# Second projection of a feed-forward block: operand loads issued three steps ahead from five buffers, and the last part's token blocks taken one at a time

## The chip, the cores and the metric

The kernel runs on one core of a Trainium2 chip. The metric is the device time of one execution in microseconds (us). The core has engines with instruction queues of their own: PE (matrix multiplies, with its weight loads), DVE, ACT and POOL (elementwise work), and SP, whose queue issues the transfers (DMA) between the chip's memory and the on-chip buffer. Each queue works strictly in the order of its list: an instruction that has to wait holds everything behind it in the same list.

## The reference

The kernel is one layer of an encoder trunk. The change touches the end of the layer, the second matrix multiply of the feed-forward block, with the residual and the layer norm behind it:

```
h = silu(x @ w_gate) * (x @ w_up)
x = LN(alpha * x + h @ w_down)        # 1024 tokens of the prompt, 128 sample tokens, D_MODEL 1024
```

All numbers are fp32. Each operand is split into a high and a low half, and each product is made of three matmuls (high by high, high by low, low by high).

## The kernel before

The second projection is `second_projection` (L1140 to L1257). It runs at the end of the program, from 1403 us of the profiled span. It uses a fast scheme for two-by-two block matrices with seven products in place of eight: for every pair of 128-row slices of the inner dimension there are seven operands of the tokens (B11, T1, T2, B22, T3, B21, T4, stored in `h_scratch` by the stage before) and seven of the weights (A11, S1, S2, S4, S3, A12, A22).

The 11 pairs are taken in five parts (`PARTS`): four of two pairs, then one of three. The tokens are in four blocks. In a part the blocks (0, 1) go through all seven steps together, then the sample tokens are done (`sample`), then the blocks (2, 3) go through the seven steps. In the last part, behind the sample, block 2 goes alone and then block 3 alone. Each step of two blocks in a part of two pairs is 12 matmuls of 128x512, a step of one block in the last part is 9.

For each step `operand` (L1146) issues the transfer of the operand into `hq` (two buffers), ACT copies it to `hh` (high half) and DVE (B11, T2, B22, B21) or POOL (T1, T3, T4) makes `hl` (low half). `hh` and `hl` have five buffers each. The step's result stands in one of two PSUM banks for each of the names x, z and w, and `add` (L1156) adds it to the sum `y` in the on-chip buffer: DVE does so at L1164, and for the w step ACT copies it to `tap` (L1161) and POOL adds it (L1162). In the last part DVE adds all of it and takes the statistics (L1168). Steps 1, 3, 5 and 7 of a block go on in the same x bank, so PE may begin such a step only when DVE has read the bank.

The weights of the next part are made beside this by `prepare` (L1103): for each pair two transfers of 512 KB into `raw` (L1108), sums on POOL (L1111 to L1114), high halves on ACT and low halves on DVE or, for A21 and A22, POOL (L1121, L1122). The odd pairs' `raw` has a single buffer, so its next transfer waits for POOL's last low half of the pair before.

`final_norm` (L1081) normalizes a finished block in the last part, on DVE, POOL and ACT, and its stores (L1097) go through SP's list too.

The order within each engine's list is fixed when the program is built. The order of SP's list decides which transfers wait behind which.

Of the kernel before, what the change touches and what calls it, by code (L numbers as in the profile page):

```python
# [9 lines left out]
F32 = mybir.dt.float32  # L10
F32R = mybir.dt.float32r
# [3 lines left out]
ALU = mybir.AluOpType  # L15
# [3 lines left out]
P = 128  # L19
# [15 lines left out]
PARTS = ((0, 2), (2, 4), (4, 6), (6, 8), (8, 11))  # L35
# [67 lines left out]
def trunk(ctx, tc, I, O):  # L103
    nc = tc.nc
    V, S, G = nc.vector, nc.scalar, nc.gpsimd
# [16 lines left out]
    def bank(name):  # L122
        return pp[name][0].tile([P, 512], F32, name=name, tag=(pp[name] + (name,))[2], bufs=pp[name][1])
# [28 lines left out]
    def mm3(out, a, b, start, stop, **kw):  # L152
        T.matmul(out, a[0], b[0], start=start, stop=False, **kw)
        T.matmul(out, a[0], b[1], start=False, stop=False, **kw)
        T.matmul(out, a[1], b[0], start=False, stop=stop, **kw)
# [77 lines left out]
    xs, hs = both[:, :1024].rearrange("p (k c) -> p k c", k=KT), both[:, 1024:]  # L233
# [672 lines left out]
    OPS = ("B11", "T1", "T2", "B22", "T3", "B21", "T4")  # L906

    h_dram = nc.dram_tensor("h_scratch", (2, len(OPS), P, PAIRS, 2, P), F32, kind="Internal").ap()
# [10 lines left out]
    def unit(c, name, dt=F32):  # L919
        return c.tile([P, 2048], dt, name=name, tag="u", bufs=14)  # L920
# [219 lines left out]
    def second_projection(f2, c, ahead, prepared, prepare):  # L1140
# [2 lines left out]
        sums = [bank("s") for _ in range(2)]  # L1143
        gb = []

        def operand(i0, i1, bs, o):  # L1146

            k, n, c = i1 - i0, len(bs), bs[0] % 2
            lo, q, hi = (f2.tile([P, 3, 2, P], t, name=x, bufs=m)[:, :k, :n]
                         for x, t, m in (("hl", F32R, 5), ("hq", F32, 2), ("hh", F32R, 5)))  # L1150
            nc.sync.dma_start(out=q, in_=h_dram[bs[0] // 2, OPS.index(o), :, i0:i1, c:c + n])
            S.copy(hi, q)  # L1152
            (G if o in ("T1", "T3", "T4") else V).tensor_tensor(lo, q, hi.bitcast(F32), op=ALU.subtract)
            return [[(hi[:, i, b], lo[:, i, b]) for i in range(k)] for b in range(n)]

        def add(b, e, half, ps, bn, which):  # L1156
            hs = slice(half * 512, half * 512 + 512)
            key = (b, e, half)
            if which == "w" and bn is None:
                t = f2.tile([P, 512], F32, name="tap", bufs=2)  # L1160
                S.copy(t, ps)  # L1161
                G.tensor_tensor(y[b, e][:, hs], y[b, e][:, hs], t, op=ALU.add)  # L1162
            else:
                V.scalar_tensor_tensor(y[b, e][:, hs], y[b, e][:, hs], 1.0 if key in y else ALPHA, ps,  # L1164
                                       op0=ALU.mult, op1=ALU.add)
            y[key] = True
            if bn is not None:
                V.bn_stats(bn[:, half], y[b, e][:, hs])  # L1168

        steps = (("x", "A11", "B11", True, (0, 0, None)),  # L1170
                 ("z", "S1", "T1", True, (1, 1, None)),
                 ("x", "S2", "T2", False, (1, 0, None)),
                 ("z", "S4", "B22", False, (1, 0, 1)),
                 ("x", "S3", "T3", False, (1, 1, 1)),
                 ("w", "A12", "B21", True, (0, 0, 0)),
                 ("x", "A22", "T4", False, (0, 1, 0)))

        def blocks(part, bs, gb):

            ws = [prepared[i] for i in range(*part)]  # L1180
            bk = {}
            bn = {(b, e): sm.tile([P, 2, 6], F32, name="bn", bufs=6) for b in bs for e in range(2)} if gb else {}
            for which, w, h, start, (e, half, fin) in steps:
                for b, hs in zip(bs, ahead.pop((bs[0] + part[0], h), None) or operand(*part, bs, h)):
                    if start:
                        bk[which, b] = bank(which)
                    ps = bk[which, b]
                    for n, wk in enumerate(ws):
                        mm3(ps, hs[n], wk[w], start and n == 0, n == len(ws) - 1, skip_group_check=not start)
                    add(b, e, half, ps, None if fin is None else bn.get((b, fin)), which)  # L1190
                    if gb and (w == "S3" or w == "A22"):
                        final_norm(y[b, fin], gb, bn[b, fin], b, fin)
                    yield

        def sample_operands(part):
            out = []
            for i in range(*part):
                q, hi, lo = (f2.tile([P, 2, P], t, name=x, bufs=2) for x, t in (("hs", F32), ("hsh", F32R), ("hsl", F32R)))
                nc.sync.dma_start(out=q, in_=hs_dram[:, i])
                split(q, hi, lo)  # L1200
                out.append((hi, lo))
            return out
# [19 lines left out]
        for n, part in enumerate(PARTS):  # L1222
            last = n == len(PARTS) - 1
            if n == 0:
                for e in range(2):
                    for b in range(2):
                        nc.sync.dma_start(out=y[b, e], in_=x2_dram[TILES[b + 4 * e]])
            if last:
                both = unit(c, "ln_gb").rearrange("p (n x) -> p n x", n=2)
                gb = [both[:, n] for n in range(2)]  # L1230
                for n in range(2):
                    nc.sync.dma_start(out=gb[n], in_=I["ln"][4 + n:5 + n, :].broadcast_to([P, D]))
            yield from blocks(part, (0, 1), gb)
            hs = sample_operands(part)
            if n == 0:
                for e in range(2):
                    for b in range(2, 4):
                        nc.sync.dma_start(out=y[b, e], in_=x2_dram[TILES[b + 4 * e]])

            while len(prepared) < min(part[1] + 1, PAIRS):  # L1240
                more()
            yield from sample(part, hs, n == 0, last)
            if last:
                ys = unit(c, "ys")[:, :1024]
                nc.sync.dma_start(out=ys, in_=x2_dram[SAMPLE])
                bn = sm.tile([P, 2, 6], F32, name="bn", bufs=6)
                for half in range(2):
                    c2 = slice(half * 512, half * 512 + 512)
                    V.scalar_tensor_tensor(ys[:, c2], ys[:, c2], ALPHA, sums[half], op0=ALU.mult, op1=ALU.add)
                    V.bn_stats(bn[:, half], ys[:, c2])  # L1250
                final_norm(ys, gb, bn, None, None)
                for b in (2, 3):
                    yield from blocks(part, (b,), gb)
                return
            while len(prepared) < PARTS[n + 1][1]:
                more()
            yield from blocks(part, (2, 3), gb)  # L1257
# [209 lines left out]
```

## Time and profile before

| | |
|---|---|
| median of 3 runs | 1707.23 us (1706.56 to 1713.33) |
| profiled execution, its own time | 1704.64 us |
| profiled execution, span | 1702.9 us |
| PE busy | 1620.7 us, 95% of the span |
| DVE, ACT, POOL busy | 67%, 40%, 29% |

The own time is 1.7 us longer than the span, and 2.6 us shorter than the median of the runs. The busy shares are averages over stages with different limits: the second projection is about 300 us long, from 1403 us, and PE has more idle time there than the average says.

### The profile page before, as it was taken

The page shows a single profiled execution, that of the slowest core. Times are in us where ns is not written, and L with a number is a line of the kernel's source. Part 1 is how long each engine was busy: PE and PEld are TensorE (multiplying, and loading weights), DVE is VectorE, ACT ScalarE, POOL GpSimd, SP SyncE. Part 2 cuts the span into 40 slices and gives each one's busy share as a digit, 9 for nine tenths or more (in the row PEclk, how much of TensorE's full clock was granted, in tenths as well). Part 3 has the DMA queues.
Part 4 walks back from the last instruction along what each step waited for, and adds up shares of the span by engine and source line. Part 5 has one row for each costly group of instructions (what it writes and reads, how often), then busy time and mean ns, then how long its engine had stood idle before and what let it go on. Part 6 is the DMA issues. An engine that isn't in the chain of part 4 may idle for free.

```text
span 1702.9 us, 24403 instructions
## 1 busy us (share of the span) xinstructions
PE 1620.7 (95%) x9065; PEld 1391.3 (82%) x9065; DVE 1134.6 (67%) x2021; ACT 674.4 (40%) x1365; POOL 495.7 (29%) x381
## 2 busy tenths in 40 slices
PE   8999999999999999999979999999999969988896
PEld 7998999999888987889877888888888857766674
DVE  6786788778488666786687454544444665767576
ACT  4543555446443544325263333323222333434321
POOL 1111111111000000000074443332333454676555
PEclk9999999999999999999998999999999988999998
DMA  7443343334974687556362333122222245333342
GB/s 239 143 160 122 102 148 104 98 118 137 314 274 154 197 278 268 198 171 236 115 205 78 104 115 117 66 74 86 95 92 96 93 164 180 105 118 118 103 146 95
DMA packets 114358, 247.91 MB, mean 146 GB/s; under 512 B 11840, under 2 KB 58048, under 8 KB 114240
## 3 DMA queue, kind: packets, MB, share of 16 engines
q1 hardware_dynamic: 114240, 246.36, 43.8%
q8 instruction: 71, 1.16, 0.3%
q14 instruction: 47, 0.39, 0.1%
HBM read 203.65 MB, written 42.60 MB: 145 GB/s over the span
## 4 chain that ended last, share of the span: by engine, by line
PE 77%; DVE 7%; DMA 6%; POOL 5%; ACT 2%; issue 2%; SPq 1%; POOLq 0%; ACTq 0%; DVEq 0%
PE a L96 48%; PE b L96 20%; PE x L96 3%; PE b L100 2%; DMA hq<-h_scratch 2%; PE z L96 1%; DVE w L1122 1%; PE s L96 1%; DMA raw<-in_w_f_dram 1%; PE w L96 1%; DVE y L1164 1%; DMA w_raw<-in_w_out_dram 1%; DMA w_raw<-in_w_fm_dram 1%; DMA w_raw<-in_w_f_dram 1%; DVE w_lo L137 1%
## 5 line engine op out<-in xcount | busy, mean ns | idle before, releaser
L137 DVE TENSOR_TENSOR w_lo<-w_raw,w_hi 128x1024 fp32r<-128x1024 f32 (+1 forms) x169 | 204.8, 1214 | 115.0 <-ACT w_hi L136 114.6
L136 ACT CAST w_hi<-w_raw 128x1024 fp32r<-128x1024 f32 (+1 forms) x169 | 174.6, 1034 | 206.1 <-PE a L96 77.4
L96 PE MATMUL a<-w_hi,q_hi 128*128 128x256 f32 (+1 forms) x576 | 197.4, 344 | 0.8 <-ACT kv_sb L270 0.7
L96 PE MATMUL a<-w_lo,q_hi 128*128 128x256 f32 (+1 forms) x576 | 196.9, 342 | 0.0
L96 PE MATMUL a<-w_hi,q_lo 128*128 128x256 f32 (+1 forms) x576 | 194.7, 338 | 0.0
L96 PE MATMUL a<-q_hi,w_hi 128*128 128x384 f32 x528 | 186.8, 354 | 7.3 <-ACT q_hi L136 4.3
L96 PE MATMUL a<-q_hi,w_lo 128*128 128x384 f32 x528 | 179.9, 341 | 0.0
L96 PE MATMUL a<-q_lo,w_hi 128*128 128x384 f32 x528 | 179.5, 340 | 0.0
L96 PE MATMUL x<-w,hh 128*128 128x512 f32 x344 | 115.0, 417 | 39.5 <-DVE y L1164 23.6
L137 DVE TENSOR_TENSOR w_lo<-a,w_hi 128x1024 fp32r<-128x1024 f32 x43 | 75.0, 1743 | 76.9 <-ACT w_hi L136 76.9
L96 PEld LDWEIGHTS a<-w_hi,q_hi 128*128 128x128 f32 x576 | 108.4, 188 | 15.6 <-ACT kv_sb L270 1.1
L96 PEld LDWEIGHTS a<-w_lo,q_hi 128*128 128x128 f32 x576 | 108.6, 189 | 13.3 <-issue 1.2
L96 PEld LDWEIGHTS a<-w_hi,q_lo 128*128 128x128 f32 x576 | 108.5, 188 | 12.7 <-issue 0.2
L96 PEld LDWEIGHTS x<-w,hh 128*128 128x128 f32 x344 | 66.6, 198 | 62.8 <-ACT hh L1152 15.7
L96 PEld LDWEIGHTS a<-q_hi,w_hi 128*128 128x128 f32 x528 | 100.5, 190 | 12.2 <-ACT q_hi L136 4.6
L699 POOL TENSOR_TENSOR rs<-rs,mhalf 128x1 f32<-128x1 f32 x18 | 17.2, 958 | 301.0 <-DVE rs L698 301.0
L96 PE MATMUL a<-T_h,w_hi 128*128 128x512 f32 x264 | 104.7, 396 | 0.0
L96 PE MATMUL a<-T_l,w_hi 128*128 128x512 f32 x264 | 104.7, 396 | 0.0
L96 PE MATMUL a<-T_h,w_lo 128*128 128x512 f32 x264 | 104.6, 396 | 0.0
L96 PEld LDWEIGHTS a<-q_lo,w_hi 128*128 128x128 f32 x528 | 100.7, 191 | 1.6 <-issue 0.9
L96 PEld LDWEIGHTS a<-q_hi,w_lo 128*128 128x128 f32 x528 | 100.2, 190 | 1.0 <-DVE w_lo L137 0.7
L1152 ACT CAST hh<-hq 128x512 fp32r<-128x512 f32 (+2 forms) x75 | 46.3, 619 | 133.2 <-DMA hq<-h_scratch 117.3
(308 smaller groups left out, 3930.4 us busy)
## 6 DMA issues: line engine op xcount, KB each, us to landing
a<-in_w_f_dram SPq DMA_DIRECT2D x44, 512.0 KB, 5.2
w_raw<-in_w_fm_dram SPq DMA_DIRECT2D x41, 512.0 KB, 3.9
h_scratch<-w_raw SPq DMA_DIRECT2D x55, 256.0 KB, 2.2
hq<-h_scratch SPq DMA_DIRECT2D x54, 256.0 KB, 2.7
w_raw<-in_w_tm_dram SPq DMA_DIRECT2D x24, 512.0 KB, 3.5
w_raw<-in_w_out_dram SPq DMA_DIRECT2D x24, 512.0 KB, 5.7
w_raw<-in_w_mq_dram SPq DMA_DIRECT2D x24, 512.0 KB, 4.2
w_raw<-in_w_mo_dram SPq DMA_DIRECT2D x24, 512.0 KB, 4.4
```

Source lines behind the costliest of these rows:

```text
L96: return self.eng.matmul(out, lhsT, rhs, **kw)
L100: return self.eng.transpose(out, in_, identity)
L136: S.copy(hi, src)
L137: V.tensor_tensor(lo, src, hi.bitcast(F32), op=ALU.subtract)
L699: G.tensor_tensor(rs, rs, mhalf[:, 0:1], op=ALU.pow)
L1122: (G if name in ("A21", "A22") else V).tensor_tensor(lo, src, hi.bitcast(F32), op=ALU.subtract)
L1152: S.copy(hi, q)
L1164: V.scalar_tensor_tensor(y[b, e][:, hs], y[b, e][:, hs], 1.0 if key in y else ALPHA, ps, op0=ALU.mult, op1=ALU.add)
```

## The change

There is one list, `wanted`, of all operands in the order in which the steps use them. At each step `operand` calls `load` for this step and the next three and `part_of` (the split into `hh` and `hl`) for this step and the next one. `hq` has five buffers of 512 elements to a partition, where there were two of 768, and `hh` and `hl` have five of 512 each in place of five of 768. In the last part the blocks 0 and 1 go singly as well, so seven transfers of 384 KB become fourteen of 192 KB.

```diff
-        def operand(i0, i1, bs, o):
-
-            k, n, c = i1 - i0, len(bs), bs[0] % 2
-            lo, q, hi = (f2.tile([P, 3, 2, P], t, name=x, bufs=m)[:, :k, :n]
-                         for x, t, m in (("hl", F32R, 5), ("hq", F32, 2), ("hh", F32R, 5)))
-            nc.sync.dma_start(out=q, in_=h_dram[bs[0] // 2, OPS.index(o), :, i0:i1, c:c + n])
-            S.copy(hi, q)
-            (G if o in ("T1", "T3", "T4") else V).tensor_tensor(lo, q, hi.bitcast(F32), op=ALU.subtract)
-            return [[(hi[:, i, b], lo[:, i, b]) for i in range(k)] for b in range(n)]
+        turns = [(part, bs) for part in PARTS[:-1] for bs in ((0, 1), (2, 3))] + [(PARTS[-1], (b,)) for b in range(4)]
+        wanted = [(*part, bs, step[2]) for part, bs in turns for step in steps][2:]
+        loaded, parted = {}, {}
+
+        def load(n):
+            if n < len(wanted) and n not in loaded:
+                i0, i1, bs, o = wanted[n]
+                k, m, c = i1 - i0, len(bs), bs[0] % 2
+                q = f2.tile([P, 512], F32, name="hq", bufs=5)[:, :k * m * P].rearrange("p (i b x) -> p i b x", b=m, x=P)
+                nc.sync.dma_start(out=q, in_=h_dram[bs[0] // 2, OPS.index(o), :, i0:i1, c:c + m])
+                loaded[n] = q
+
+        def part_of(n):
+            if n < len(wanted) and n not in parted:
+                i0, i1, bs, o = wanted[n]
+                k, m, q = i1 - i0, len(bs), loaded[n]
+                hi, lo = (f2.tile([P, 512], F32R, name=x, bufs=5)[:, :k * m * P].rearrange("p (i b x) -> p i b x", b=m, x=P)
+                          for x in ("hh", "hl"))
+                S.copy(hi, q)
+                (G if o in ("T1", "T3", "T4") else V).tensor_tensor(lo, q, hi.bitcast(F32), op=ALU.subtract)
+                parted[n] = [[(hi[:, i, b], lo[:, i, b]) for i in range(k)] for b in range(m)]
+
+        used = [0]
+
+        def operand():
+            n = used[0]
+            used[0] += 1
+            for x in range(n, n + 4):
+                load(x)
+            for x in range(n, n + 2):
+                part_of(x)
+            return parted.pop(n)
...
-                for b, hs in zip(bs, ahead.pop((bs[0] + part[0], h), None) or operand(*part, bs, h)):
+                for b, hs in zip(bs, ahead.pop((bs[0] + part[0], h), None) or operand()):
...
-            yield from blocks(part, (0, 1), gb)
+            for bs in ((0,), (1,)) if last else ((0, 1),):
+                yield from blocks(part, bs, gb)
```

SP's list at the change from the first part to the second, before. 13433, 13455, 13477 and 13497 are B11, T1, T2 and B22 of the second part's blocks (0, 1); raw2_13594 and raw2_13646 are the weights of pairs 4 and 5.

```order
L1151 DMA hq_13433<-h_scratch 128x512
L1151 DMA hq_13455<-h_scratch 128x512
L1108 DMA raw2_13646<-in_w_f2_dram 128x1024
L1108 DMA raw2_13594<-in_w_f2_dram 128x1024
L1151 DMA hq_13477<-h_scratch 128x512
L1151 DMA hq_13497<-h_scratch 128x512
L1108 DMA raw2_13594<-in_w_f2_dram 128x1024
L1108 DMA raw2_13646<-in_w_f2_dram 128x1024
```

The same place in the changed kernel. 13442, 13464, 13486 and 13506 are B22, T3, B21 and T4 of the same blocks, 13526 is B11 of the blocks (2, 3); raw2_13604 and raw2_13656 are pairs 4 and 5.

```order
L1164 DMA hq_13442<-h_scratch 128x512
L1223 DMA hs_13990<-hs_scratch 128x256
L1164 DMA hq_13464<-h_scratch 128x512
L1108 DMA raw2_13656<-in_w_f2_dram 128x1024
L1108 DMA raw2_13604<-in_w_f2_dram 128x1024
L1164 DMA hq_13486<-h_scratch 128x512
L1164 DMA hq_13506<-h_scratch 128x512
L1108 DMA raw2_13604<-in_w_f2_dram 128x1024
L1164 DMA hq_13526<-h_scratch 128x512
L1108 DMA raw2_13656<-in_w_f2_dram 128x1024
```

The operands stand three places earlier against the weights: T2 and B22 were behind the first two weight transfers and are ahead of them now, and pair 4's second weight transfer is still behind two operand loads. On ACT, DVE and POOL the rows of these parts keep their order.

SP's list near the end of the last part, before. `out` rows are stores of finished blocks (13036 and 13037 of blocks 0 and 1, 13042 of block 2, `ys` of the sample); 15122, 15139, 15156, 15172, 15189, 15220 and 15238 are the seven operands of block 3 in the order of the steps.

```order
L1097 DMA out_0_dram<-y_13037 128x512 x2
L1095 DMA out_0_dram<-ys_14949 128x512 x2
L1151 DMA hq_15122<-h_scratch 128x3x128
L1151 DMA hq_15139<-h_scratch 128x3x128
L1151 DMA hq_15156<-h_scratch 128x3x128
L1151 DMA hq_15172<-h_scratch 128x3x128
L1097 DMA out_0_dram<-y_13042 128x512 x2
L1151 DMA hq_15189<-h_scratch 128x3x128
L1151 DMA hq_15220<-h_scratch 128x3x128
L1151 DMA hq_15238<-h_scratch 128x3x128
```

The same place in the changed kernel. 15058 and 15074 are the last two operands of block 2; 15091, 15122, 15140, 15173, 15190, 15207 and 15223 are the seven of block 3.

```order
L1164 DMA hq_15058<-h_scratch 128x3x128
L1164 DMA hq_15074<-h_scratch 128x3x128
L1164 DMA hq_15091<-h_scratch 128x3x128
L1097 DMA out_0_dram<-y_13041 128x512 x2
L1164 DMA hq_15122<-h_scratch 128x3x128
L1164 DMA hq_15140<-h_scratch 128x3x128
L1097 DMA out_0_dram<-y_13037 128x512 x2
L1095 DMA out_0_dram<-ys_15001 128x512 x2
L1164 DMA hq_15173<-h_scratch 128x3x128
L1164 DMA hq_15190<-h_scratch 128x3x128
L1164 DMA hq_15207<-h_scratch 128x3x128
L1164 DMA hq_15223<-h_scratch 128x3x128
L1097 DMA out_0_dram<-y_13042 128x512 x2
```

Block 3's first three loads stood behind the sample's stores and stand ahead of them now; its last three stood behind block 2's first stores and now stand ahead of those too.

## Rows read from the trace of the kernel before

**Rows 1.** Windows by stage: length; busy us of PE, PEld, DVE, ACT, POOL; clock; DMA.

```profile
1403.10:1469.50 66.40, 58.40 (x222) 44.95 (x222) 44.88 (x56) 24.41 (x45) 38.70 (x27) 0.91 0.47 152
1469.50:1522.10 52.60, 46.70 (x192) 35.60 (x192) 35.20 (x47) 19.82 (x36) 33.66 (x23) 1.00 0.36 115
1522.10:1575.00 52.90, 48.45 (x192) 37.78 (x192) 35.83 (x47) 19.66 (x36) 33.64 (x23) 0.94 0.36 115
1575.00:1613.10 38.10, 32.60 (x138) 25.92 (x138) 22.22 (x31) 12.88 (x23) 21.33 (x15) 1.00 0.38 114
1613.10:1654.60 41.50, 39.86 (x162) 31.51 (x163) 32.15 (x53) 12.12 (x20) 23.98 (x18) 0.96 0.43 136
1654.60:1692.40 37.80, 32.23 (x127) 23.87 (x125) 26.87 (x49) 8.14 (x14) 19.15 (x17) 0.95 0.28 95
```

**Rows 2.** Waits from 1395 to 1703 us: total us, times, longest.

```profile
ACT hh L1152 <- DMA hq<-h_scratch: 117.3, 31, 9.6
PE x L96 <- DVE y L1164: 23.6, 14, 5.6
```

**Rows 3.** PE's timeline, 1403 to 1470 us: start, duration, instruction, idle time before it.

```profile
1403.14 2.07 PE L96 MATMUL x<-w,hh 128*128 128x512 f32 x4 [15.24 <-ACT hh L1152]
...
1425.08 0.63 PE L96 MATMUL x<-w,hh 128*128 128x512 f32 x2
...
1432.21 0.70 PE L96 MATMUL x<-w,hh 128*128 128x512 f32 x2 [1.35 <-DVE y L1164]
...
1439.36 1.22 PE L96 MATMUL z<-w,hh 128*128 128x512 f32 x2 [2.70 <-DVE y L1164]
```

**Rows 4.** Timelines of ACT, POOL and SP around the first change of part.

```profile
1434.95 0.62 ACT L1152 CAST hh<-hq 128x512 fp32r<-128x512 f32 x1 [1.09 <-DMA hq<-h_scratch]
1435.48 1.66 ACT L1121 CAST w<-s 128x512 fp32r<-128x512 f32 x3
...
1442.42 0.81 SPq L1108 DMA_DIRECT2D raw<-in_w_f_dram  x2
...
1445.75 0.90 SPq L1108 DMA_DIRECT2D raw<-in_w_f_dram  x2
...
1451.67 1.72 POOL L1111 TENSOR_TENSOR s<-raw 128x512 f32<-128x512 f32 x1
```

**Rows 5.** Timelines of SP, ACT, POOL and PE around the second change of part.

```profile
1497.11 0.90 SPq L1108 DMA_DIRECT2D raw<-in_w_f_dram  x2
...
1500.60 0.62 ACT L1152 CAST hh<-hq 128x512 fp32r<-128x512 f32 x1 [5.27 <-DMA hq<-h_scratch]
...
1501.78 1.28 POOL L1162 TENSOR_TENSOR y<-y,tap 128x512 f32<-128x512 f32 x1 [5.08 <-ACT tap L1161]
1503.05 1.70 POOL L1111 TENSOR_TENSOR s<-raw 128x512 f32<-128x512 f32 x1
...
1522.13 0.73 PE L96 MATMUL x<-w,hh 128*128 128x512 f32 x2 [1.65 <-DVE y L1164]
```

**Rows 6.** DMA issues from 1497.05 to 1497.40 us: size, us to landing.

```profile
raw<-in_w_f_dram SPq DMA_DIRECT2D x1, 512.0 KB, 5.9
```

**Rows 7.** Timelines of POOL and PE at the change to the last part.

```profile
1606.51 1.28 POOL L1111 TENSOR_TENSOR s<-raw 128x512 f32<-128x512 f32 x1 [0.97 <-DMA raw<-in_w_f_dram]
...
1613.19 1.19 PE L96 MATMUL x<-w,hh 128*128 128x512 f32 x2 [5.57 <-DVE y L1164]
```

**Rows 8.** Timelines of PE, SP and ACT in the last part.

```profile
1660.07 0.74 PE L96 MATMUL x<-w,hh 128*128 128x512 f32 x2 [1.06 <-DVE y L1164]
...
1680.35 0.70 PE L96 MATMUL z<-w,hh 128*128 128x512 f32 x2 [1.77 <-DVE y L1164]
...
1685.82 0.71 PE L96 MATMUL x<-w,hh 128*128 128x512 f32 x2 [1.84 <-DVE y L1164]
...
1678.72 5.11 SPq L1151 DMA_DIRECT2D hq<-h_scratch  x3
...
1681.84 0.51 ACT L1152 CAST hh<-hq 128x384 fp32r<-128x384 f32 x1 [7.03 <-DMA hq<-h_scratch]
```

More of the change, by code (lines that the diff above doesn't have):

```diff
@@ L1144, in second_projection @@
         gb = []
-        def operand(i0, i1, bs, o):
-            k, n, c = i1 - i0, len(bs), bs[0] % 2
-            lo, q, hi = (f2.tile([P, 3, 2, P], t, name=x, bufs=m)[:, :k, :n]
-                         for x, t, m in (("hl", F32R, 5), ("hq", F32, 2), ("hh", F32R, 5)))
-            nc.sync.dma_start(out=q, in_=h_dram[bs[0] // 2, OPS.index(o), :, i0:i1, c:c + n])
-            S.copy(hi, q)
-            (G if o in ("T1", "T3", "T4") else V).tensor_tensor(lo, q, hi.bitcast(F32), op=ALU.subtract)
-            return [[(hi[:, i, b], lo[:, i, b]) for i in range(k)] for b in range(n)]
+        steps = (("x", "A11", "B11", True, (0, 0, None)),
+                 ("z", "S1", "T1", True, (1, 1, None)),
+                 ("x", "S2", "T2", False, (1, 0, None)),
+                 ("z", "S4", "B22", False, (1, 0, 1)),
+                 ("x", "S3", "T3", False, (1, 1, 1)),
+                 ("w", "A12", "B21", True, (0, 0, 0)),
+                 ("x", "A22", "T4", False, (0, 1, 0)))
@@ L1168, in add @@
                 V.bn_stats(bn[:, half], y[b, e][:, hs])
[L1170 to L1176, printed above, removed]
         def blocks(part, bs, gb):
```

## The prediction

> **What bounds the kernel now.** PE is 95% busy over the span, so I first look for the stages where it is not. The windows by stage [rows 1] show it: from 1469.5 us a part of two pairs takes 52.6 us, for 192 matmuls. At full clock 24 matmuls run from 1425.08 to 1430.86 us, where PE falls idle [rows 3], 0.24 us each, so 192 are 46 us, and each such part holds some 6.6 us of stall. The first part with its surroundings is worse, and the last part (1613.1 to 1692.4, 289 matmuls, 69.4 us of work) takes 79.3.
>
> Next, who is waited for [rows 2]. ACT stands 117 us waiting for operand transfers (`hq`), far the longest entry, yet PE waits for something else: 23.6 us for DVE's y additions. So a late `hq` costs time only where ACT, behind it DVE, and behind that a y addition come late in turn. I follow that by place, since every list is in order: a y addition on DVE stands behind low halves of operands and of weights, and those behind ACT and POOL.
>
> *First part, blocks (2, 3).* Here `hq` decides. PE stalls 1.35 and 2.70 us for y, and behind the second the first two matmuls take 1.22 us against 0.63 at 1425.08 [rows 3]: the clock fell to its half level for a while. ACT waits for `hq` until 1434.95 and only then makes the weights' halves (1435.48). POOL's low halves follow, and SP can issue the next weights at 1442.42 and, behind two operand loads, at 1445.75; POOL's first sum over them is at 1451.67 [rows 4].
>
> *Second and third change of part.* Two chains arrive together. POOL idles 5.08 us for a `tap` that ACT could not copy because it waited 5.27 us for `hq`; that addition ends at 1503.06. But the weight transfer issued at 1497.11 [rows 5] takes 5.9 us to land [rows 6], so at 1503.0, and POOL's sum begins at 1503.05. From that sum to the end of the stalls (1522.13) POOL, ACT and DVE work through the weights, with PE's y additions between.
>
> *Change to the last part.* POOL's sum waits for `raw` itself (0.97 us, 1606.51) and PE restarts 6.7 us later, after its longest gap, 5.57 us [rows 7].
>
> *Last part.* PE stalls 1.06, 1.77 and 1.84 us [rows 8], among smaller ones. The last comes from the list of SP: three loads of block 3 are issued from 1678.72 on, behind stores, ACT gets the first at 1681.84 after 7.03 us, then DVE splits it and adds y.
>
> **The change part by part.** The order of ACT, DVE and POOL in the parts of two pairs is as before, and so is the arithmetic; what moves is SP's list, three steps.
>
> *Start.* The 15.24 us ahead of 1403.14 [rows 3] stay: ACT waits there for the first operand, behind the loads of `y`, and those still stand ahead of it. Gain 0.
>
> *First part.* Loads come early, so both stalls and the half clock go, and ACT can make the weights' halves when PE has finished S1, at 1430.9, not 1435.5: 4.6 us earlier. POOL's low halves and the first weight transfers then come at about 1437. The second ones were also held by an operand's buffer, until 1445.75. In the new order pair 4's second transfer still stands behind two operand loads (B21 and T4), but those use buffers freed by halves of B11 and T1, of which only T1's, on POOL, comes near; I put it at 1438.5. Plus 5.9 us [rows 6] that is 1444.4, and POOL's sum, behind the two `tap` additions, at about 1445.5 in place of 1451.67. All behind it follows: 6.2 us, of which I take 6.0. Bounds: 0, if the transfer that was issued at 1445.75 does not move; 6.7, if the sum is made at 1445.0.
>
> *Second and third change.* The `hq` wait goes, but the weight transfer does not: it is tied to POOL's low halves of the pair before. It gains only what it waited behind the operand's buffer, about 0.6 us of which I count 0.5 each, so 1.0 in all. PE's early gaps close and come back as one longer gap, ahead of the same weights. Bounds: 0 and 5.1 (half of the 5.08 that POOL idles, 2.54, at either change, if the weights land earlier too because fewer operand loads share the way).
>
> *Change to the last part.* The operands around `raw` are half as large. I take 1.0 of the 5.57; bounds 0 and 2.0.
>
> *Last part.* 79.3 less 69.4 is 9.9 us, of which about 1.3 belong to the half clock just behind 1613.19 and stay (the first two matmuls take 1.19 there [rows 7], 0.56 more than at 1425.08; 1.3 is an estimate for the stretch). 8.6 can go: block 3's loads now stand ahead of block 2's stores. Against it, blocks taken singly have less cover: between two steps that go on in one x bank stands one step of 9 matmuls (2.2 us), not three. In blocks 2 and 3 such a wait is 1.06 where nothing of `hq` was late [rows 8]. I charge one such stall for blocks 0 and 1 together: 8.6 - 1.1 is 7.5. DVE does not become the bound by its load: 32.15 and 26.87 us of 79.3, plus 1.5 us as fourteen small halves cost more than seven large [rows 1]. Bounds: 1.0, if blocks 0 and 1 lose as much as blocks 2 and 3 did (37.8 less 30.2 for 126 matmuls, 7.6), to 8.6.
>
> The end behind PE's last matmul, 10.5 us of norm and store, stays.
>
> **Sum.** 6.0 + 1.0 + 1.0 + 7.5 is 15.5. The profiled execution's own time, 1704.64, becomes 1689.1. The median is 2.6 above that execution, so I forecast 1691.7.
>
> **A rule that speaks against it.** The trace shows a gap of 2.70 us with the half clock behind it, and one of 5.57 too [rows 3, 7]; at 1522.13, behind 1.65 us, two matmuls take 0.73 and the clock stays up [rows 5]. So closing several short gaps and leaving one long one can cost clock. The Trainium skill ("TensorE: Matmul & The Clock Gate", section "HAM oscillation — how this bites in real kernels") says the same of loops: a wait for a transfer sends the engine back to half clock, and the stretch behind it pays, each time anew. By that rule the second and third change would each lose what the first matmuls after 1613.19 lose, 1.3 us, and more if the half clock lasts as it does behind 1439.36.
>
> **The rivals.** *The first part does not move.* If the weights' second transfer or another queue place holds POOL's sum at 1451.7, the stalls only shift, and 9.5 remains: 1697.7, or 1701 if the last part gives half. For it: in the later parts just this happens. Against: there the transfer was issued without a late operand ahead of ACT, in the first part the whole chain starts 4.6 us late.
>
> *Operands decide at every change.* If the weights land earlier once fewer operand loads contend, 2.54 in place of 0.5 at each of two changes and 2.0 in place of 1.0 at the last: 1691.7 - 4.1 - 1.0 is 1686.6, and 1681.5 with the whole 5.08 at both. For it: both chains end within 0.05 us of each other in rows 5, so neither is seen alone.
>
> *The clock falls at the long gaps.* 1.3 to 3 us at up to three places: 1693 to 1700. Against: behind the gap POOL's chain, not PE, sets the end, and a slower PE is partly hidden.
>
> *Slower: the x bank.* With single blocks each of 12 returns to an x bank (three in each of four blocks) must find DVE's y addition done within 2.2 us, and DVE may hold it with a norm or a low half. If every return waits 2 us, that is 24 us in place of the 8.6 that can go: 15.4 lost in the last part. With the 8.0 gained ahead of it the time is 1714.6, with nothing gained there 1722.6. It is slower by over 0.5% from 2.1 us a return in the first case ((8.6 + 8.0 + 8.5) / 12), from 1.4 us in the second. The returns in blocks 2 and 3 that are seen to wait cost 1.06 to 1.84 and most cost nothing, which speaks against it.
>
> **How the numbers follow.** 0.5%, about what a measurement of this kernel can tell from no change, is 8.5 us: faster means under 1698.7. The forecast (1687 to 1697) has 0.48, operands deciding everywhere 0.14, the clock 0.14 (0.11 of it still faster), the first part unmoved 0.18 (a third of it faster, since the last part would more likely give less than more), the x bank 0.06. That gives faster 0.79, same 0.15, slower 0.06. The range leaves out the x bank, the far end of the unmoved first part, and a gain above 24 us: 1683 to 1701.
>
> **What would show it.** Right: ACT's wait for `hq` falls from 117 to under 40 us after 1410 us; the stalls of 1.35 and 2.70 and the half clock behind them are gone; POOL's first sum behind the first part comes some 6 us earlier, the distance between such sums of consecutive parts stays within 1 us of 51.4 (1451.67 to 1503.05); the stalls at a change stand in one piece of 3 to 5 us; blocks 2 and 3 run in under 33 us. Wrong: the sums' distances shrink by 2 us or more (operands decided), or do not move at all; PE waits for y at the third, fifth or seventh step of blocks 0 and 1.

## The result, and the profile after

The changed kernel takes 1695.64 us (median of 7 runs, 1692.0 to 1700.13), the kernel before 1708.47 (7 runs, 1706.56 to 1713.33). The ratio is 0.9925, with a 95% interval from 0.9912 to 0.9938: 12.8 us less, where 15.5 were forecast.

The two profiled executions differ by less, 1695.47 against 1704.64. PE reaches the projection's first step behind the start at 1408.64 us in the changed kernel and at 1403.14 before [rows 3], and the gap ahead of it is nearly the same. So the changed kernel's profiled execution had lost 5.1 us before that gap began. I don't put this down to the change: over all kernels below the first step lies between 1396 and 1409 us, and with six buffers, in two kernels that differ only in `hq`, 5.45 us apart. From here to the end of the span it is 299.8 us before and 285.0 in the changed kernel, 14.8 less. So I compare stages, not whole executions.

PE's timeline of the changed kernel, the main rows with idle time ahead of them (start, duration, instruction, idle time):

```profile
1408.64 2.07 PE L96 MATMUL x<-w,hh 128*128 128x512 f32 x4 [15.64 <-ACT hh L1173]
...
1441.77 0.73 PE L96 MATMUL z<-w,hh 128*128 128x512 f32 x2 [1.48 <-DVE y L1196]
...
1455.75 0.73 PE L96 MATMUL x<-w,hh 128*128 128x512 f32 x2 [2.23 <-DVE y L1196]
...
1469.64 0.73 PE L96 MATMUL x<-w,hh 128*128 128x512 f32 x2 [1.08 <-DVE y L1196]
...
1506.52 0.73 PE L96 MATMUL x<-w,hh 128*128 128x512 f32 x2 [2.65 <-DVE y L1196]
...
1521.49 0.73 PE L96 MATMUL x<-w,hh 128*128 128x512 f32 x2 [1.65 <-DVE y L1196]
...
1558.39 0.73 PE L96 MATMUL x<-w,hh 128*128 128x512 f32 x2 [2.67 <-DVE y L1196]
...
1608.99 1.19 PE L96 MATMUL x<-w,hh 128*128 128x512 f32 x2 [4.12 <-DVE y L1196]
...
1633.93 0.71 PE L96 MATMUL z<-w,hh 128*128 128x512 f32 x2 [1.28 <-DVE y L1196]
...
1673.99 0.70 PE L96 MATMUL z<-w,hh 128*128 128x512 f32 x2 [1.26 <-DVE y L1196]
```

The 1.35 and 2.70 of the first part [rows 3] are one stall of 1.48 now, and no half clock follows: matmuls in pairs take 0.73 there, not 1.22. At the change to the second part 2.23 and 1.08 are left. Not shown above: between the 2.65 and the 1.65 of the second change PE also waits 0.23 and 0.75 us, and 1.09 behind the 2.67 of the third. The 5.57 ahead of the last part [rows 7] is 4.12. In the last part there is a new stall of 1.28 in block 1; of those in blocks 2 and 3 [rows 8] one of 0.31 and one of 1.26 are left.

The waits of the changed kernel from 1395 us on (who waited for whom: total us, times, longest):

```profile
ACT hh L1173 <- PE x L96: 46.2, 20, 4.1
...
PE x L96 <- DVE y L1196: 15.7, 8, 4.1
...
ACT hh L1173 <- DMA hq<-h_scratch: 9.9, 1, 9.9
```

ACT's 117.3 us of waiting for operands [rows 2] have become one wait at the start. What ACT waits for now is PE, that is, a free `hh` buffer. POOL's first sums over new weights show who comes last at a change of part:

```profile
1452.03 1.30 POOL L1111 TENSOR_TENSOR s<-raw 128x512 f32<-128x512 f32 x1 [2.38 <-DMA raw<-in_w_f_dram]
1453.29 1.26 POOL L1194 TENSOR_TENSOR y<-y,tap 128x512 f32<-128x512 f32 x1
...
1502.81 1.29 POOL L1111 TENSOR_TENSOR s<-raw 128x512 f32<-128x512 f32 x1 [2.81 <-DMA raw<-in_w_f_dram]
...
1554.68 1.28 POOL L1111 TENSOR_TENSOR s<-raw 128x512 f32<-128x512 f32 x1 [2.83 <-DMA raw<-in_w_f_dram]
...
1601.81 1.29 POOL L1111 TENSOR_TENSOR s<-raw 128x512 f32<-128x512 f32 x1 [3.46 <-DMA raw<-in_w_f_dram]
```

At each of the four POOL now stands waiting for the weights alone. Before, POOL's sum at 1503.05 came right behind a late `tap` addition [rows 5].

For all kernels the stages are measured between the starts of the sample's matmuls, which have a fixed place between the blocks (0, 1) and the next ones of each part. So the stretch from one sample to the next holds a change of part. From here on the first part is the stretch from sample 1 to 2, with the first change; the third part is the one from sample 2 to 3, with the second change, and the fourth the one from sample 3 to 4, with the third change. In us, worked out from the timelines:

```
                 start to  sample 1  sample 2  sample 3  sample 4    sample 5
                 sample 1  to 2      to 3      to 4      to 5 (last) to last matmul
before             16.3      57.2      52.6      52.9      62.0        47.9
changed            16.0      52.1      51.9      50.8      63.0        39.8
singles only       16.4      56.3      53.2      52.7      66.9        46.6
five, no list      16.1      52.3      51.9      52.1      61.1        39.8
hq four            16.6      51.8      51.9      51.6      61.3        39.8
raw two            16.5      61.1      48.9      51.1      63.3        39.8
pair last, six     15.9      52.3      48.2      47.9      61.1        45.8
hq three           16.9      52.9      52.0      51.7      64.2        39.6
raw two, late      15.8      49.7      48.9      48.9      63.0        39.8
load one           16.0      54.5      51.8      51.7      61.1        39.8
six                16.5      51.4      47.9      48.0      63.9        39.9
split six          15.8      49.9      48.3      47.9      63.5        39.9
six, hq first      18.9      47.9      48.0      47.9      63.5        39.9
```

### The profile page after: what moved, and what is told of

Its sections match the earlier page's. It is cut to its first block, busy times and chain, and to the rows that moved or that the text cites. A ratio compares the mean times of both kernels' runs of the same rounds, so it can differ in the third digit from the quotient of the medians.

```text
span 1693.6 us, 24454 instructions
## 1 busy us (share of the span) xinstructions
PE 1618.2 (96%) x9065; PEld 1392.1 (82%) x9065; DVE 1127.7 (67%) x2025; ACT 677.5 (40%) x1372; POOL 497.1 (29%) x384
## 4 chain that ended last, share of the span: by engine, by line
PE 78%; DVE 7%; DMA 5%; POOL 5%; issue 3%; ACT 2%; SPq 1%; POOLq 0%; ACTq 0%; DVEq 0%
PE a L96 47%; PE b L96 20%; PE x L96 4%; PE b L100 2%; PE z L96 2%; PE s L96 1%; PE w L96 1%; DMA raw<-in_w_f_dram 1%; DMA w_raw<-in_w_f_dram 1%; DVE w L1122 1%; POOL s L1111 1%; DMA w_raw<-in_w_mv_dram 1%; DVE w_lo L137 1%; ACT w L1121 1%; DVE y L1196 1%
## 5 line engine op out<-in xcount | busy, mean ns | idle before, releaser
L1173 ACT CAST hh<-hq 128x512 fp32r<-128x512 f32 (+1 forms) x82 | 47.0, 582 | 91.5 <-PE x L96 46.2
```

## The experiments

**Singles only.** The kernel before, with one line of the change.

```diff
-            yield from blocks(part, (0, 1), gb)
+            for bs in ((0,), (1,)) if last else ((0, 1),):
+                yield from blocks(part, bs, gb)
```

> The kernel before, with blocks 0 and 1 singly in the last part and nothing else: two operand buffers, no list. My theory (the loads' early place gives the gain, singles give nothing): the second projection, from its first matmul to the end of the span, takes 299.8 us before and 285.0 in the changed kernel; here 300 to 304, since 14 loads go through two buffers in the last part; the ratio to before is 1.000 to 1.003. Rival (singles spread the norms and give the last part its 5 us): 294 to 296, ratio 0.997.

Measured: 1710.4 us against 1705.06 for the kernel before, ratio 1.0031 (1.0019 to 1.0043). From the fourth sample to the fifth it takes 66.9 us in place of 62.0. Two rows of its PE timeline in the last part and its wait for operands:

```profile
1647.78 0.71 PE L96 MATMUL x<-w,hh 128*128 128x512 f32 x2 [3.70 <-DVE y L1164]
...
1689.56 0.80 PE L96 MATMUL x<-w,hh 128*128 128x512 f32 x2 [3.14 <-DVE y L1164]
```

```profile
ACT hh L1152 <- DMA hq<-h_scratch: 124.6, 37, 9.6
```

Fourteen loads through two buffers wait more often (37 times for 31), and single blocks cannot cover it. The rival falls: singles alone are a loss, of 5.3 us by the medians and of 3.0 in the profiled projection (302.8 us against 299.8).

**Five buffers, no list.** Singles and five operand buffers, but each step still asks for its own operand and splits it then.

```diff
-            lo, q, hi = (f2.tile([P, 3, 2, P], t, name=x, bufs=m)[:, :k, :n]
-                         for x, t, m in (("hl", F32R, 5), ("hq", F32, 2), ("hh", F32R, 5)))
+            lo, q, hi = (f2.tile([P, 512], t, name=x, bufs=m)[:, :k * n * P].rearrange("p (i b x) -> p i b x", b=n, x=P)
+                         for x, t, m in (("hl", F32R, 5), ("hq", F32, 5), ("hh", F32R, 5)))
```

> Singles and five operand buffers of 512, but no list: each step still asks for its own operand only. The program's lists show the loads as early against the weights as in the changed kernel, since a load is placed when its buffer is free. My theory (SP's order, which the buffers set): 284 to 287 us for the second projection, ratio to before 0.992. Rival (asking three steps ahead and splitting one ahead is what matters): 292 to 298 us, ratio 0.996 to 0.999.

Measured: 1693.42 us, ratio 0.993 (0.991 to 0.995), 284.5 us from the first step to the end, all stages within 2 us of the changed kernel. So the list, the three steps ahead and the split one step ahead give nothing that five buffers don't give by themselves. SP issues the loads in nearly the same order: at the first three changes of part the fourth weight transfer stands one operand load earlier than in the changed kernel. What the program asks for early or late matters little here; with the buffers free, the loads come early.

**Four, and three, operand buffers.** The changed kernel with one number changed.

```diff
-                q = f2.tile([P, 512], F32, name="hq", bufs=5)
+                q = f2.tile([P, 512], F32, name="hq", bufs=4)
```

> The changed kernel with four operand buffers in place of five. My theory: the operands are still early enough everywhere, 284 to 287 us and ratio to before 0.992, as with five. Rival (the depth of the loads decides): 287 to 291 us. It is also the control for the next one.

> The changed kernel with three operand buffers. My theory (the operand must only be there when ACT comes to it, and one landing takes 2.7 to 6 us, about one to two steps of 2.8 us): most of the gain is there with three, 285 to 289 us, ratio 0.992 to 0.995. Rival (three steps ahead are needed): 290 to 296 us, ratio 0.996 to 0.998.

Measured: four give 1693.73 us, ratio 0.9928 (0.991 to 0.9946), the same as five. Three give 1696.83, ratio 0.9946 (0.9934 to 0.9959), 288.1 us from the first step to the end, at the upper side of what I expected. ACT's waits for operands are back in part, with three:

```profile
ACT hh L1173 <- DMA hq<-h_scratch: 67.4, 18, 9.8
```

They cost little in the parts of two pairs (52.0 and 51.7 us), where the weights hold POOL's sums anyway. The stage of the single blocks 0 and 1 takes 64.2 us, where it is 61.3 with four and 63.0 with five.

The run with four also shows a change of part with the clock down. Its PE timeline there:

```profile
1502.40 1.22 PE L96 MATMUL x<-w,hh 128*128 128x512 f32 x2 [2.68 <-DVE y L1196]
...
1517.39 0.73 PE L96 MATMUL x<-w,hh 128*128 128x512 f32 x2 [0.93 <-DVE y L1196]
```

Behind a gap of 2.68 us the clock is at its half level (1.22 us for two), where the changed kernel's 2.65 left it up (0.73, at 1506.52). Both stages take 51.9 us: the slower matmuls shorten the later stalls (0.93 for 1.65, and the 0.23 and 0.75 between are gone).

**Loads one step ahead.** `range(n, n + 2)` in place of `range(n, n + 4)` for `load`.

> The changed kernel with the loads asked for one step ahead in place of three, five buffers kept. The program's lists put the loads at the same places against the weights from the second part on, and only the first call issues six, not eight. My theory (buffers set the place): 284 to 287 us, ratio 0.992 to 0.993. Rival (the three steps): 288 us or more, ratio over 0.995.

Measured: 1695.53 us, ratio 0.9941 (0.9927 to 0.9954), 286.1 us. The 286.1 us are what my theory expected; the ratio lies between the two expectations, and its interval overlaps that of the changed kernel. The first part takes 54.5 us and not 52.1, the other stages are within 2 us of the changed kernel's. The run without any list had 52.3 in the first part, so the three steps are not needed for it. What the 2.4 us are is seen in the trace: the stalls come to some 1.1 us more, and behind one of 2.34 the clock falls (0.57 from 1439 to 1443 us, where the changed kernel and the one without a list have 1.00 from 1438 to 1450).

**Two weight buffers for all later pairs.** The weights' transfers then wait neither for POOL's last low half of the pair before nor for a place among the other weights.

```diff
-            raw = (at.tile([P, 2, 1024], F32, name="raw2") if at else
+            raw = (at.tile([P, 2, 1024], F32, name="raw2", bufs=2) if at else
...
-                prepare(i, f2 if i % 2 else None)
+                prepare(i, f2)
...
-                q = f2.tile([P, 512], F32, name="hq", bufs=5)
+                q = f2.tile([P, 512], F32, name="hq", bufs=4)
```

> The changed kernel with four operand buffers and the raw weights of all later pairs in two buffers of their own, so that a pair's transfers no longer wait for POOL's last low half of the pair just before. My theory (at each change of part the late weights' landing decides, POOL waits 2.4 to 3.5 us for it): POOL's first sum comes 2 to 3 us earlier at three or four changes, second projection 275 to 280 us, ratio to before 0.987 to 0.989. Rival (operands or DVE decide): within 1 us of the one with four buffers.

Measured: 1690.58 us, ratio 0.9914 (0.9898 to 0.993), and 292.5 us from the first step to the end, not 275 to 280. Two effects that I had not seen hide each other. PE's gap at the start is half as long: the second part's first weights, whose sums and halves stood in POOL's and ACT's lists beside the last work of the stage before, now come after it (POOL's first sum of them at 1413.91, in the changed kernel at 1388.14, ahead of PE's first step):

```profile
1396.24 2.07 PE L96 MATMUL x<-w,hh 128*128 128x512 f32 x4 [7.79 <-ACT hh L1173]
```

And those weights come late: the first part takes 61.1 us in place of 51.8. The third part, 48.9 for 51.9 with four buffers, is what the theory gives. The fourth, 51.1 for 51.6, is not, and there the clock was down. Its stalls are those of the third (2.03 and 1.11 us, for 2.03 and 1.41), and the granted clock is 0.50 from 1553 to 1557 us, where it is 1.00 from 1504 to 1508 in the third. In the next run both parts take 48.9 us with the clock up. So here the half clock costs about 2.2 us at a change of part:

```profile
1553.55 1.22 PE L96 MATMUL x<-w,hh 128*128 128x512 f32 x2 [1.11 <-DVE y L1196]
```

I mended the experiment so that only the later weights have the two buffers:

```diff
-                prepare(i, f2 if i % 2 else None)
+                prepare(i, f2 if i > 2 else None)
```

> Two weight buffers as in the run before this, with four operand buffers, but only from the third part's weights on, so that the second part's come as in the changed kernel. The run before gained at the later changes of part (48.9 and 51.1 us a part in place of 51.9 and 51.6) and at the start (gap 7.8 us), and lost 9 us in the first part, where the weights of the second came late. If the weights' landing costs what POOL waits for it, the first part is 52, the next ones 49 to 51, second projection 279 to 282 us, ratio 0.990 to 0.991; if the stalls only move to another place of DVE's list, 283 to 285 us, ratio 0.992 to 0.993.

Measured: 1686.86 us, ratio 0.9884 (0.9872 to 0.9897), 277.5 us, below the 279 to 282 that I expected. Parts of 49.7, 48.9 and 48.9. POOL's sum waits for no transfer, and PE's stall at a change of part is another one:

```profile
1492.46 1.78 POOL L1111 TENSOR_TENSOR s<-raw 128x512 f32<-128x512 f32 x1
```

```profile
1501.87 0.70 PE L96 MATMUL x<-w,hh 128*128 128x512 f32 x2 [2.02 <-ACT w L1121]
...
1505.16 0.73 PE L96 MATMUL x<-w,hh 128*128 128x512 f32 x2 [1.42 <-DVE y L1196]
```

So in the changed kernel the weights' landing counts: with it early, a part gets 2 to 3 us shorter. POOL's wait (2.38 to 2.83) is no measure of that, though the numbers are near each other: the first sum of the second change begins 18.07 us behind sample 2, where it is 26.05 in the changed kernel. Of these 8 us only 3 reach PE, which then waits for ACT's halves and for y.

**The blocks 0 and 1 together again.** The changed kernel with the last part's first two blocks in pairs, the fourteen small loads kept, six buffers of each kind.

```diff
-            for bs in ((0,), (1,)) if last else ((0, 1),):
-                yield from blocks(part, bs, gb)
+            yield from blocks(part, (0, 1), gb)
```

> The changed kernel, but in the last part the blocks 0 and 1 go through the steps together again; their fourteen transfers and splits stay (six buffers of 512 each, so that a step's two halves fit). Only the order of PE's steps and of the norms differs. My theory (the loads' place gives the gain, a single block has too little cover for y): from the sample of the fourth part to that of the last 60 to 62 us in place of 63.0, from there to PE's end 41 to 43 in place of 39.8, as the norms of both blocks come together; second projection 283 to 286, ratio to before 0.992. Rival (singles are part of the gain): 288 to 291 us, ratio 0.995.

Measured: 1688.62 us, ratio 0.99 (0.9887 to 0.9913). The last stretch takes 45.8 us, longer than I expected, and the third and fourth parts take 48.2 and 47.9, which pairing in the last part cannot do: the sixth buffers, brought in only to make room, had an effect of their own. Two more runs took the two apart.

**Six buffers.** The changed kernel with six of each (hq, hh, hl), and with six of hh and hl alone.

```diff
-                hi, lo = (f2.tile([P, 512], F32R, name=x, bufs=5)
+                hi, lo = (f2.tile([P, 512], F32R, name=x, bufs=6)
```

> The changed kernel with six buffers of 512 each for hq, hh and hl in place of five. The run with the blocks 0 and 1 paired had six as well, and its third and fourth parts took 48.2 and 47.9 us, not 51.9 and 50.8, while its last stretch took 45.8 and not 39.8. If the six buffers made the parts shorter and the pairing the last stretch longer, this one has parts of 52, 48 and 48 us, 61 to 63 up to the last sample and 39.8 behind it: second projection 276 to 279 us, ratio 0.986 to 0.988. If the pairing had to do with both, 284 us and 0.992.

> Six buffers for hh and hl, five for hq as in the changed kernel. If a free place for the split halves is what the parts of 52 us still waited for (POOL's halves of weights come behind it, and the next weights behind those), the third and fourth parts are 48 us as with six of each, ratio 0.986 to 0.988. If it is the sixth hq buffer, they are 51 to 52 us, ratio 0.992.

Measured: six of each 1683.65 us, ratio 0.9878 (0.9858 to 0.9898); six of the split halves alone 1682.1, ratio 0.987 (0.9848 to 0.9892). Both have parts of 48 us behind the first. It is the sixth place for a split half; whether for `hh` or for `hl` no run tells. In the changed kernel POOL's rows of the second change read like this:

```profile
1490.28 1.60 POOL L1174 TENSOR_TENSOR hl<-hq,hh 128x512 fp32r<-128x512 f32 x1 [11.26 <-ACT hh L1173]
1491.85 3.04 POOL L1122 TENSOR_TENSOR w<-raw,w 128x512 fp32r<-128x512 f32 x2
1494.82 1.31 POOL L1174 TENSOR_TENSOR hl<-hq,hh 128x512 fp32r<-128x512 f32 x1
```

With six of each, which runs 4.7 us earlier from the start on:

```profile
1480.97 1.29 POOL L1174 TENSOR_TENSOR hl<-hq,hh 128x512 fp32r<-128x512 f32 x1 [7.37 <-ACT hh L1173]
...
1486.05 2.54 POOL L1122 TENSOR_TENSOR w<-raw,w 128x512 fp32r<-128x512 f32 x2 [3.78 <-ACT w L1121]
...
1497.58 1.73 POOL L1111 TENSOR_TENSOR s<-raw 128x512 f32<-128x512 f32 x1
```

POOL's half of an operand comes a step earlier and no longer stands ahead of the weights' halves. These end at 1488.6, 84.7 us behind the first step, where the changed kernel's end at 1494.9, 86.3 behind; the next transfers go 1.6 us earlier, and POOL's sum waits for nothing.

But that is not what makes the part 4 us shorter. Counted from sample 2, the sum begins 25.70 us behind it, and 26.05 in the changed kernel; with six of the halves alone it begins later, at 26.58, and waits 0.84 us for the weights, and the part is 48.3 us all the same:

```profile
1501.67 1.28 POOL L1111 TENSOR_TENSOR s<-raw 128x512 f32<-128x512 f32 x1 [0.84 <-DMA raw<-in_w_f_dram]
```

What differs is DVE's list. In the changed kernel the 13th y addition behind sample 2, which PE waits for with its 2.65 us, stands behind a low half of a weight sum, and so behind ACT and POOL's sum:

```profile
1504.78 1.09 DVE L1122 TENSOR_TENSOR w<-s,w 128x512 fp32r<-128x512 f32 x1 [2.63 <-ACT w L1121]
1505.79 0.67 DVE L1196 SCALAR_TENSOR_TENSOR y<-y,x 128x512 f32<-128x512 f32 x1
```

With six of each the 13th and the 14th both stand ahead of the first such half:

```profile
1498.10 0.67 DVE L1196 SCALAR_TENSOR_TENSOR y<-y,x 128x512 f32<-128x512 f32 x1
...
1502.29 0.67 DVE L1196 SCALAR_TENSOR_TENSOR y<-y,x 128x512 f32<-128x512 f32 x1
1502.89 1.78 DVE L1122 TENSOR_TENSOR w<-s,w 128x512 fp32r<-128x512 f32 x2
```

PE's stalls in the third part are then 0.58 and 0.72 us, where the changed kernel has 5.3 us of them. I read this from the traces; no run changes DVE's order alone.

The six buffers also give the comparison that the run before was meant for. With blocks 0 and 1 together the last two stages are 61.1 + 45.8 = 106.9 us, singly 63.9 + 39.9 = 103.8. PE's timeline in the last part, blocks together:

```profile
1636.31 0.73 PE L96 MATMUL s<-w,hsh 128*128 128x512 f32 x2 [1.13 <-ACT hsh L136]
...
1637.84 0.51 PE L96 MATMUL s<-w,hsl 128*128 128x512 f32 x1 [0.79 <-DVE rs L1084]
...
1646.97 1.22 PE L96 MATMUL x<-w,hh 128*128 128x512 f32 x2 [2.31 <-DVE y L1200]
```

With loads in time, singles are a gain of 3 us: in pairs, two norms come together (`rs` is a row of theirs), and the sample and block 2 stall. Without, they are a loss.

**Six buffers, operands ahead of y.** The first four loads stand ahead of y's at the start of the projection.

```diff
             if n == 0:
+                for x in range(4):
+                    load(x)
                 for e in range(2):
```

> Six buffers of each, and the first four operand loads are asked for ahead of the loads of y (blocks 0 and 1) at the start of the projection. PE stands 15 us there. If the operand behind y on the queue decides, the gap falls by 1.5 to 3 us and the ratio by 0.001 to 0.002 against the run with six; if y itself or the stage before decides, the gap stays at 15 us and the ratio equal.

Measured: 1680.43 us, ratio 0.9859 (0.9842 to 0.9877), the fastest of all, though its interval overlaps that of six without it. PE's gap at the start is 10.07 us, and PE takes the step with a fresh bank (w) first:

```profile
1397.99 1.22 PE L96 MATMUL w<-w,hh 128*128 128x512 f32 x2 [10.07 <-ACT hh L1173]
1399.16 0.79 PE L96 MATMUL w<-w,hl 128*128 128x512 f32 x1
1399.75 1.05 PE L96 MATMUL w<-w,hh 128*128 128x512 f32 x2
1401.46 1.22 PE L96 MATMUL x<-w,hh 128*128 128x512 f32 x2 [0.66 <-DVE y L1196]
```

The shorter gap is in part paid back: PE has less to do until the y additions come, at half clock (1.22 us for two). From the end of the stage before, the gap's beginning, to the first sample it is 29.0 us (1387.92 to 1416.87) against 30.9 with six buffers alone (1389.54 to 1420.48). So about 2 us of the 15 at the start were the operand's place behind y, as expected. The first part, 47.9 us for 51.4, gained more: PE's stalls there are 0.58 and 0.72 us, the pair that the later changes have with six buffers, in place of 0.51, 1.48, 0.34 and 2.69.

## Why the prediction was right, step by step

*The direction, the range and the places held.* The projection became 14.8 us shorter, where the sum of the steps said 15.5. That the sum came so near is in part luck: the terms below are off by 0.6 and 1.4 us one way and by 1.8 the other. One sign failed: the stalls at a change do not stand in one piece of 3 to 5 us, but in two to four, the longest of 2.23 to 2.67. Blocks 2 and 3 run in 31.7 us, under the 33 that I had named.

*The start.* Forecast 0; the gap is 15.64 for 15.24. Right, though the last experiment shows that it need not have been so long.

*The first part.* Forecast 6.0. From the first step to the second sample it is 73.5 us before and 68.1 now, so 5.4. POOL's sum comes 43.4 us behind the first step and not 48.5: 5.1 earlier, where I had said 6.2. ACT's halves of the weights begin 27.8 us behind the first step, just where I had put them (1430.9); what I had too early is what follows. SP's rows in the changed kernel show it. The first transfers are issued 34.9 us behind the first step, where I had said 33.9 (1437). Pair 4's second transfer is issued at 1445.67, 37.0 us behind the first step, where I had put it at 35.4 (1438.5 from 1403.14); the sum is forecast 42.4 behind it and measured 43.4:

```profile
1443.53 0.81 SPq L1108 DMA_DIRECT2D raw<-in_w_f_dram  x2
1444.44 1.18 SPq L1164 DMA_DIRECT2D hq<-h_scratch  x2
1445.67 0.44 SPq L1108 DMA_DIRECT2D raw<-in_w_f_dram  x1
```

I had also said that POOL keeps its order and that the sum stands behind both `tap` additions. It does not: before, both stood ahead of the sum at 1451.67 [rows 4], and now one stands behind it (1453.29, above). The rows before:

```profile
1448.71 1.29 POOL L1162 TENSOR_TENSOR y<-y,tap 128x512 f32<-128x512 f32 x1 [3.84 <-ACT tap L1161]
1450.39 1.32 POOL L1162 TENSOR_TENSOR y<-y,tap 128x512 f32<-128x512 f32 x1 [0.39 <-ACT tap L1161]
```

The first-part rival (the sum stays where it was) falls with this.

*Second and third change.* Forecast 0.5 each, from a weight transfer that hardly moves; measured 0.7 and 2.1. The distances between POOL's sums, 50.8 and 51.9 us, are within the 1 us of 51.4 that I had named. The wait is the one that was forecast, POOL standing for the weights alone, and with the weights earlier (two later weight buffers) the parts do get shorter. The rival that operands decide at every change falls: no operand is late in the changed kernel, and yet the stalls are there. But the forecast took the weights' landing for the whole bound, and it is not: with six split halves the sum begins as late behind the sample as here and the part is 4 us shorter, by the place of the y additions in DVE's list. The term was too small for the third change: from the sum to PE's restart at 1572.28 it is 17.6 us, and 18.7 at the second change (19.1 before, to 1522.13 [rows 5]). Why is not shown.

*Change to the last part and the last part.* Forecast 1.0 and 7.5, 8.5 in all; measured 7.1 over the two last stages, and 0.4 went again behind the last matmul. This is the term that was too large. The gap ahead of the last part became 1.45 us shorter, and blocks 2 and 3 with the sample 8.1, about the 8.6 that could go. Blocks 0 and 1 lost 2.5 us, not 1.1: one stall of 1.28 for y, as charged, and a longer half clock. From 1608.99 on the matmuls stay at the half level until 1613.8, 4.8 us, where before it was 2.8, from 1613.19 to 1616. At half the speed 2.0 us more are a loss of about 1 us, by an estimate:

```profile
1612.97 1.05 PE L96 MATMUL z<-w,hh 128*128 128x512 f32 x2
```

Blocks 2 and 3 run without the longest stall of [rows 8], since block 3's loads stand ahead of block 2's stores.

*The clock.* Behind the 4.12 us ahead of the last part the clock is at its half level, for 2.0 us longer than before. At the third change it fell too, a little behind the gap of 2.67 us at 1558.39:

```profile
1561.01 1.05 PE L96 MATMUL z<-w,hh 128*128 128x512 f32 x2
```

At the second change, behind 2.65, it did not (0.73 at 1506.52). Yet the stage with the third change is the shorter one, 50.8 us against 51.9, and with four buffers the second change takes 51.9 us with the clock down too. So in the changed kernel the rival that long gaps cost clock falls as a loss of time at the changes of part and holds, by the estimate of 1 us, ahead of the last one. It is no rival that falls everywhere: with two weight buffers for all pairs the half clock costs 2.2 us at the third change. The Trainium skill ("TensorE: Matmul & The Clock Gate", section "HAM oscillation — how this bites in real kernels") says of loops that a wait for a transfer sends the engine back to half clock, and the stretch behind it pays. The clock at 1608.99 and 1561.01 agrees with it, behind waits for y; whether the time follows differs from place to place here.

*What I had wrong without its costing anything.* I took the list for the cause of the loads' place. It is the number of buffers: the run without a list has nearly the same order and the same time. And I took the weights' raw buffer for all that bounds the changes of part. The split halves' buffers do so too: one more of them gives at least as much as a second raw buffer, and, as the rows above show, not by way of earlier weights.

*The x bank.* Of the 12 returns to an x bank in the last part none shows a wait: the three stalls left are at z steps. A row of DVE ahead of 1673.99 shows what does hold y, the norm's wait for POOL:

```profile
1671.12 0.74 DVE L1089 SCALAR_TENSOR_TENSOR y<-y,mv,ln_gb 128x512 f32<-128x512 f32 x1
1672.29 0.95 DVE L1086 SCALAR_TENSOR_TENSOR nb<-mv,rs 128x1 f32<-128x1 f32 x1 [0.44 <-POOL rs L1085]
1673.17 0.68 DVE L1196 SCALAR_TENSOR_TENSOR y<-y,z 128x512 f32<-128x512 f32 x1
```

*What stays open.* What DVE's order alone is worth at a change of part; why the run with loads one step ahead stalls longer in the first part while that without a list does not; and how much of the operands' earlier place at the start is the queue's, since the second run with a short gap there (two weight buffers) reached it another way.

## What to carry to other kernels

When a chain of waits shows a late transfer, look at what comes second: here, at the second change, the weights landed within 0.1 us of the end of the late operand's chain, so an earlier operand gave 0.7 us at that place, and 5.4 in the first part, where the weights' transfers moved with it. Count buffers before writing a schedule: with buffers enough, the order came nearly the same without one. When a sixth buffer helps, look for where: the long wait of ACT for a free `hh` hardly changed with it (46.2 to 42.5 us), POOL's sum came at nearly the same place, and the 4 us a part lay, as far as the rows show, in two y additions that moved ahead of a waiting half in DVE's list. A smaller unit of work (single blocks) pays only after its inputs are in time; alone it lost what it later gained.

## What the runs showed of the hardware that was not expected

Gaps of nearly one length left PE's clock in different states: behind 2.65 us it stayed at its full level (0.73 us for two matmuls), behind 2.67 it fell only after some matmuls at full speed, behind 2.68 the first two already took 1.22. The length alone does not order them: in the run with loads one step ahead the first two took 1.22 behind 2.56 us (1504.97), and without a list they took 0.73 behind 2.85 (1557.86). Transfers of half the size brought no wait that the trace shows: with fourteen loads of 192 KB in place of seven of 384 KB, and buffers enough, ACT waits for an operand once in the whole projection, at the start.
